# A second stacked query tile in place of a 64-row operand in the score matmuls of a banded-attention trunk

## Chip, cores and metric

The kernel runs on one core of a Trainium2 chip. The metric is device time in microseconds of one execution, taken as the median of several. Before the change it is 2212.74 us (three runs, 2210.71 to 2214.65).

## What is computed

One layer of a hybrid encoder over 2048 tokens of width 1024, in float32. Only the attention part matters here: eight heads of 64 channels, where each chunk of 64 tokens attends to itself and to the eight chunks before it.

```python
h = rms_norm(x, norm1_g); p = h @ w_in          # q, k, v, conv and pool inputs
q = rms_norm(q, q_norm_g); k = rms_norm(k, k_norm_g)
scores = einsum('bnqhd,bnkhd->bnhqk', qc, kb) * d ** -0.5
scores = where(valid, scores + bias, NEG_INF)
out = einsum('bnhqk,bnkhd->bnqhd', softmax(scores), vb)
mix = concat([out, y_conv, y_pool]);  x = x + mix @ w_out
x = x + square(relu(rms_norm(x) @ w_mlp1)) @ w_mlp2
```

The norm gains of q and k and the relative bias are scaled by 8 in the inputs, so scores are large and their products are made from split operands.

## The kernel before, in words

The tokens are handled in four blocks of 512 (`block(b, ...)`, line 332), and after them the MLP runs over everything (from line 720). A block first projects q, k and v (`project`, line 349), then runs attention, into which `weave` (line 73) mixes other matmuls: the output projection of the block before and the conv and pool projections of this block. `InOrder` (line 54) fixes the order of TensorE's instructions to the order in which they are written. The other engines' orders come from the Tile framework's scheduler, which follows priorities and its own timeline, and all DMAs on the data path are issued by SyncE (SP), in one queue.

Each float32 operand of a matmul is split into a rounded high part and the rest: hi + lo. A general product takes three matmuls (`mm3`, lines 157 to 160: hi*hi, hi*lo, lo*hi). The scores do it in two. For a head h = 2*hp + j, the keys are stacked on 128 partitions in the tile `kx`: on the head's own 64 rows the high part, on the other 64 rows the low part. `qs` stacks the queries the other way round: low part on the own rows, high part on the others. So the matmul of line 471, over 128 rows, gives q_lo*k_hi + q_hi*k_lo. Line 472 adds q_hi*k_hi with the 64 own rows of the unstacked tile `qhi` and the 64 own rows of `kx`.

`prep(hp)` (line 390) makes these tiles for a pair of heads. TensorE transposes k and q into PSUM (line 395), ScalarE writes the high part (`khi` line 399, `qhi` line 402), VectorE the low part (`klo` line 400, `qlo` line 403). Stacking is done by DMAs: the keys go to the DRAM tensor `kd` in four stores a pair (line 412) and come back as `kx` for this block and the one before (line 415); the queries go from SBUF to SBUF into `qs` in two DMAs a head (line 418). `prep` is a generator: `attention` (line 523) advances it after the first head's second, third and fourth query tile of the pair before, and `early` (line 436) makes the first pair during the v projection.

A unit of attention is one head's query tile of 128 rows, 32 units in a block. `scores` (line 460) makes the scores of up to 640 keys in PSUM: in block 0 of 128, 256, 384 or 512 keys in one bank (two matmuls), in blocks 1 to 3 always of 640 keys in two banks of 320 (four matmuls). VectorE adds the bias and takes the maximum (line 475), ScalarE the exponential (line 481). `flip` transposes the probabilities a unit later (line 492), and `values` multiplies them with v another unit later (line 507). So 3*32*4 + 32*2 = 448 score matmuls are issued, half of them by line 472.

The pool `hd` holds the tiles of the heads: `khi`, `klo` and `qlo` in one buffer each, `qhi` in two, `qs` and `kx` in two.

Of the kernel before, what the change touches and what calls it, by code (L numbers as in the profile page):

```python
# [8 lines left out]
F32 = mybir.dt.float32  # L9
F32R = mybir.dt.float32r  # L10
# [8 lines left out]
P = 128  # L19
# [7 lines left out]
TB = 512  # L27
# [16 lines left out]
ORDERED = ("PE",)  # L44
# [5 lines left out]
def follow(tc, ins, earlier):  # L50
    tc.add_manual_dep(ins, earlier, mybir.DependencyInfo(mybir.DependencyClass.NoSync, mybir.DependencyReason.DATA), reason="order")


class InOrder:
    """Instructions traced between two calls of mark() keep their order on the engines of ORDERED."""

    def __init__(self, tc):
        nc = tc.nc
# [4 lines left out]
    def mark(self):  # L63
        new = self.tc.nc.cur_bb.bb.instructions[self.seen :]
        self.seen += len(new)
        for ins in new:
            if ins.engine in self.engines:
                if ins.engine in self.last:
                    follow(self.tc, ins, self.last[ins.engine])
                self.last[ins.engine] = ins.name  # L70
# [20 lines left out]
def trunk(ctx, tc, xT, cols, cinv, w_qkv, w_cp, w_out, w1, w2, nbias, pool_w, outT):  # L91
    nc = tc.nc
    sc, ve, te, gp, sy = nc.scalar, nc.vector, nc.tensor, nc.gpsimd, nc.sync
# [12 lines left out]
    hd = high.enter_context(tc.tile_pool(name="hd", bufs=2, side="right"))  # L106

    def pd(name, tag="d"):
        if tag == "d":
            return psd.tile([P, 512], F32, tag="d", name=name)  # L110
        return psa.tile([P, 512], F32, tag=tag, bufs=3 if tag == "t" else 1, name=name)

    def pbig(name, tag):
        return psa.tile([P, 2, 512], F32, tag=tag, bufs=1, name=name)
# [17 lines left out]
    kd = dram.tile([H, P, S], F32, name="kd")  # L132
# [8 lines left out]
        return w.rearrange("p s (a b) -> p s a b", a=shape)  # L141

    class Ahead:
        """Weights of a list of loads, each brought in some places before its use."""

        def __init__(self, loads):
            self.loads, self.ready = iter(loads), []
# [23 lines left out]
        ve.tensor_tensor(out=r, in0=r, in1=t, op=ALU.mult)  # L171
        return r

# [1 line left out]
    def scratch(name):  # L175
        return scr.tile([P, 512], F32, tag="s", name=name)

# [154 lines left out]
    def block(b, prev_out):  # L332
        t0 = b * TB
# [56 lines left out]
        def prep(hp):  # L390
            nat = {}
            for nm in "kq":
                tp = pd(f"t{nm}{b}_{hp}", TK)
                for i in range(NT):
                    te.transpose(tp[:, i * P : (i + 1) * P], nrm[nm][:, i, hp * P : (hp + 1) * P], ident)
                hi = hd.tile([P, TB], F32R, tag=nm + "hi", bufs=2 if nm == "q" else 1, name=f"{nm}hi{b}_{hp}")
                lo = hd.tile([P, TB], F32R, tag=nm + "lo", bufs=1, name=f"{nm}lo{b}_{hp}")
                if nm == "k":
                    sc.copy(hi, tp)
                    ve.tensor_tensor(out=lo, in0=tp, in1=hi.bitcast(F32), op=ALU.subtract)  # L400
                else:
                    sc.activation(hi, tp, AF.Copy, scale=qgs)
                    ve.scalar_tensor_tensor(out=lo, in0=tp, scalar=qgs, in1=hi.bitcast(F32), op0=ALU.mult, op1=ALU.subtract)
                nat[nm] = (hi, lo)
                yield
            res = []
            for j in range(2):
                h = 2 * hp + j
                rows = slice(64 * j, 64 * j + 64)
                orow = slice(64 - 64 * j, 128 - 64 * j)  # L410
                for part, r in ((0, rows), (1, orow)):
                    sy.dma_start(kd[h, r, t0 : t0 + TB], nat["k"][part][rows].bitcast(F32))
                kx = hd.tile([P, 2 * TB], F32R, tag="kx", bufs=2, name=f"kx{b}_{h}")
                first = 0 if b else TB
                sy.dma_start(kx[:, first:].bitcast(F32), kd[h, :, t0 - TB + first : t0 + TB])
                qs = hd.tile([P, TB], F32R, tag="qs", bufs=2, name=f"qs{b}_{h}")
                for part, r in ((1, rows), (0, orow)):
                    sy.dma_start(qs[r].bitcast(F32), nat["q"][part][rows].bitcast(F32))
                vp = None
                if b:  # L420
                    vp = hd.tile([P, NT, 2, HD], F16, tag="vp", bufs=2, name=f"vp{b}_{h}")
                    sy.dma_start(vp.rearrange("p t s d -> p (t s d)"), vd[(b - 1) % 2, h])
                bi = hd.tile([P, 640], F32, tag="bias", bufs=2, name=f"b{b}_{h}")
                sy.dma_start(bi, bd[h])
                res.append((kx, qs, nat["q"][0][rows], rows, vp, bi))
            return res

        if b == 0:
# [7 lines left out]
        def early():  # L436
            nrm["k"] = normalize(ack, "k")
            yield
            first.extend((yield from prep(0)))
            yield  # L440
# [14 lines left out]
        sc.copy(R, rb)  # L455
        mix = po.tile([P, 2, KT, TB], F32R, tag="mix", name=f"mix{b}")

# [1 line left out]
        def scores(u, st):  # L459
            hp, j, i = u  # L460
            h = 2 * hp + j
            kx, qs, qh, rows, vp, bi = st["heads"][j]
            lo_t = max(0, 4 * b + i - 4) - (4 * b - 4)
            nk = (4 + i + 1 - lo_t) * P
            ne = 1 if nk <= 512 else 2
            hk = nk // ne
            c0 = lo_t * P
            s = pbig(f"s{b}_{h}_{i}", "s")
            for e in range(ne):
                ks = slice(c0 + e * hk, c0 + (e + 1) * hk)  # L470
                te.matmul(s[:, e, :hk], qs[:, i * P : (i + 1) * P], kx[:, ks], start=True, stop=False)  # L471
                te.matmul(s[:, e, :hk], qh[:, i * P : (i + 1) * P], kx[rows, ks], start=False, stop=True)  # L472
            sb = hd.tile([P, 640], F32, tag="sb", bufs=2, name=f"sb{b}_{h}_{i}")
            nmx = sm.tile([P, 1], F32, tag="nmx", bufs=4, name=f"nm{b}_{h}_{i}")
            ve.tensor_tensor_reduce(  # L475
                out=sb[:, :nk].rearrange("p (e k) -> p e k", e=ne),
                in0=s[:, :ne, :hk],
                in1=bi[:, 640 - nk :].rearrange("p (e k) -> p e k", e=ne),
                scale=-1.0, scalar=3.0e38, op0=ALU.add, op1=ALU.min, accum_out=nmx,
            )  # L480
            exps.append(sc.activation(sb[:, :nk], sb[:, :nk], AF.Exp, bias=nmx, scale=-1.0, accum_out=st["l"][:, i, j : j + 1]))  # L481
            return sb, lo_t, nk, vp
# [40 lines left out]
        def attention(first):  # L523
# [4 lines left out]
            for u in units + [None, None]:  # L528
                if u:
                    hp, j, i = u  # L530
                    if j == 0 and i == 0:
                        st = {"heads": ready}
                        st["l"] = sm.tile([P, NT, 2], F32, tag="l", name=f"l{b}_{hp}")
                    got = (u, st, *scores(u, st))
                else:
                    got = None
                yield 1
                if done and (u is None or (j == 1 and i == NT - 1)):
                    finish(*done)
                    done = None  # L540
                flipping = flip(*scored) if scored else None
                if flipped:
                    done = values(*flipped) or done
                flipped, scored = flipping, got
                yield 1
                if u and j == 0 and hp < H // 2 - 1:
                    if i == 1:
                        steps = prep(hp + 1)
                    if i in (1, 2):
                        next(steps)  # L550
                        yield GAP
                    elif i == 3:
                        try:
                            next(steps)
                        except StopIteration as e:
                            ready = e.value
            finish(*done)
            yield 0

# [1 line left out]
        def dense(g):  # L561
            t = pd(f"cp{b}_{g}")
            for half in range(2):
                w = weights.next()
                for kk in range(4):
                    k = half * 4 + kk
                    mm3(t, w[:, 0, kk], w[:, 1, kk], xgs[k][:, 0], xgs[k][:, 1], k == 0, k == KT - 1)
                    if kk % 2 and k < KT - 1:
                        yield
            return t  # L570
# [76 lines left out]
                mapped(j, mh)  # L647
            yield from steps

# [1 line left out]
        acc2 = po.tile([P, TB], F32, tag="acc2", name=f"acc2{b}")  # L651

        halves = [(d, half) for d in range(KT) for half in (1, 0)]
# [60 lines left out]
    for b in range(NB):  # L714
        prev_out = block(b, prev_out)
# [1 line left out]
    high.close()  # L717
    pm0 = ctx.enter_context(tc.tile_pool(name="pm0", bufs=2, space=PSUM, side="right"))

# [1 line left out]
    xp = ctx.enter_context(tc.tile_pool(name="xp", bufs=28, side="right"))  # L721
    wp = ctx.enter_context(tc.tile_pool(name="wp", bufs=WOPS, side="right"))
    rp = ctx.enter_context(tc.tile_pool(name="rp", bufs=RAWS, side="right"))
# [195 lines left out]
    for n, u in enumerate(units):  # L919
        kind, tb, c, i = u  # L920
# [84 lines left out]
```

## Time and profile before

| | |
|---|---|
| runs | 2212.74 us median, 2210.71 to 2214.65 |
| profiled execution, span from first to last instruction | 2207.5 us (the page gives no other time for it) |
| TensorE busy | 2134.6 us, 97% |
| VectorE, ScalarE, GpSimd busy | 1596.8, 1154.1, 895.8 us |
| score matmuls, line 471, busy (all forms) | 224 instructions, first at 82.9 us, last at 911.5 us |
| DMA, share of the 16 engines | 41.3% |

PE is TensorE's matmuls, PEld its weight loads (which can overlap matmuls), DVE is VectorE, ACT ScalarE, POOL GpSimd, SPq SyncE's queue. A busy time of PE adds up instructions that overlap in the pipeline, so what a matmul costs is read from the distance between the starts of neighbours, not from its own length. The four attention stretches lie at about 81 to 174, 251 to 424, 500 to 674 and 749 to 915 us.

### The profile page before, as it was taken

The numbers are of one execution on the slowest core, as the hardware profiler recorded it, in microseconds if no ns is written. First come the engines' busy times: TensorE is split into PE (matmuls) and PEld (weight loads), VectorE is DVE, ScalarE is ACT, GpSimd is POOL, SyncE is SP. The second block draws the span as 40 slices with busy tenths as digits, with TensorE's granted clock in tenths as the row PEclk, the third lists the DMA queues.
The fourth block names the chain that finished last, engine by engine and source line by source line (L and its number), as shares of the span: only waits on it lengthen the run. The fifth ranks groups of instructions, "written<-read, shape, count | busy, mean of one in ns | idle before, by whom it ended". The sixth has DMA issues, their size and how long they took to land.

```text
span 2207.5 us, 31819 instructions
## 1 busy us (share of the span) xinstructions
PE 2134.6 (97%) x11136; PEld 1266.0 (57%) x11136; DVE 1596.8 (72%) x2401; ACT 1154.1 (52%) x2163; POOL 895.8 (41%) x693
## 2 busy tenths in 40 slices
PE   8999999999999999979999979999999999999998
PEld 6777777787777777754444434444444444444443
DVE  7677556755666556797848898767877487687685
ACT  6455455635555555545646436446256464463550
POOL 4233144402211012155636556446656355363463
PEclk9999999999999999999999999999999999999999
DMA  8664665446745576352111451115521111112123
GB/s 291 184 175 144 190 218 180 145 150 201 222 145 156 168 220 182 126 196 77 55 61 58 155 189 58 58 58 203 174 76 58 59 57 61 56 52 67 58 87 114
DMA packets 156562, 285.91 MB, mean 130 GB/s; under 512 B 18545, under 2 KB 25841, under 8 KB 156401
## 3 DMA queue, kind: packets, MB, share of 16 engines
q1 hardware_dynamic: 156400, 283.88, 41.3%
q8 instruction: 87, 1.43, 0.3%
q14 instruction: 75, 0.61, 0.1%
HBM read 236.09 MB, written 39.32 MB: 125 GB/s over the span
## 4 chain that ended last, share of the span: by engine, by line
PE 65%; DVE 12%; POOL 6%; issue 6%; DMA 6%; ACT 4%; SPq 0%; POOLq 0%; DVEq 0%; ACTq 0%
PE b_d L782 18%; PE b_u L782 11%; PE a L158 4%; PE a L160 4%; PE a L159 4%; PE s L472 3%; PE cp L158 3%; PE o L158 3%; PE pt L492 2%; PE s L471 2%; PE cp L159 2%; PE cp L160 2%; DMA r_d<-w 2%; PE o L160 2%; PE o L159 2%
## 5 line engine op out<-in xcount | busy, mean ns | idle before, releaser
L782 PE MATMUL b_d<-ft_u,s_d 128*128 128x512 f16 x1152 | 264.9, 379 | 5.8 <-DVE ft_u L733 4.3
L782 PEld LDWEIGHTS <-s_u 128*128 128x128 f16 x1536 | 150.8, 98 | 202.2 <-issue 22.4
L782 PEld LDWEIGHTS <-s_d 128*128 128x128 f16 x1536 | 150.4, 98 | 191.2 <-issue 12.5
L782 PEld LDWEIGHTS <-a_d 128*128 128x128 f16 x1152 | 114.2, 99 | 158.8 <-issue 27.1
L782 PEld LDWEIGHTS <-a_u 128*128 128x128 f16 x1152 | 113.1, 98 | 146.1 <-issue 11.9
L782 PE MATMUL b_d<-fb_u,a_d 128*128 128x512 f16 x768 | 183.7, 379 | 0.5 <-DVE acc L890 0.5
L481 ACT ACTIVATE sb<-sb,nm 128x640 f32<-128x640 f32 (+4 forms) x128 | 97.6, 762 | 142.2 <-DVE nm L475 136.3
L890 DVE TENSOR_TENSOR acc<-acc,b_d 128x512 f32<-128x512 f32 x176 | 119.4, 682 | 62.5 <-PE b_d L782 62.4
L207 POOL TENSOR_TENSOR acc<-acc,sq 128x512 f32<-128x512 f32 x56 | 80.5, 1438 | 197.8 <-ACT sq L206 157.0
L158 PE MATMUL a<-wq,xg 128*128 128x512 f32 x384 | 152.4, 402 | 8.4 <-ACT wq L139 8.1
L160 PE MATMUL a<-wq,xg 128*128 128x512 f32 x384 | 154.1, 402 | 1.5 <-DVE xg L343 1.5
L159 PE MATMUL a<-wq,xg 128*128 128x512 f32 x384 | 153.4, 399 | 0.0
L475 DVE CUSTOM_DVE_ANT_0 sb<-s,b 128x640 f32<-128x640 f32 (+4 forms) x128 | 94.4, 738 | 77.2 <-PE s L472 75.2
L782 PE MATMUL b_u<-xt,s_u 128*128 128x512 f16 x576 | 132.5, 385 | 10.1 <-DVE xt L733 6.7
L494 DVE SCALAR_TENSOR_TENSOR pp<-pt,pp 128x384 f16<-128x384 f32 (+1 forms) x224 | 102.8, 485 | 49.9 <-ACT pp L493 49.5
L139 POOL CAST wc<-rwc 128x512 fp32r<-128x512 f32 x64 | 40.2, 628 | 237.7 <-PE cp L160 127.9
L284 POOL TENSOR_TENSOR pq<-pq,pq 128x512 bf16<-128x512 bf16 x32 | 38.6, 1205 | 219.4 <-ACT pq L281 219.4
L782 PE MATMUL b_u<-zt,s_u 128*128 128x512 f16 x576 | 126.9, 379 | 0.0
L754 POOL TENSOR_TENSOR s_u<-s_u,r_u 128x512 f32<-128x512 f32 x32 | 43.8, 1370 | 201.8 <-DVE s_u L736 200.4
L736 DVE SCALAR_TENSOR_TENSOR a_u<-r_u,sw,a_u 128x512 f16<-128x512 f32 x96 | 102.5, 1069 | 21.5 <-ACT a_u L735 18.8
L735 ACT ACTIVATE a_u<-r_u,sw 128x512 f16<-128x512 f32 x96 | 68.8, 719 | 93.2 <-PE b_d L782 49.5
L158 PE MATMUL o<-mix,wo 128*128 128x512 f32 x256 | 111.2, 435 | 4.0 <-DVE xo L673 4.0
(267 smaller groups left out, 5314.6 us busy)
## 6 DMA issues: line engine op xcount, KB each, us to landing
r_u<-w SPq DMA_DIRECT2D x128, 256.0 KB, 2.6
r_d<-w SPq DMA_DIRECT2D x128, 256.0 KB, 2.7
rwq<-w_qkv SPq DMA_DIRECT2D x96, 256.0 KB, 2.8
pr<-w SPq DMA_DIRECT2D x64, 256.0 KB, 3.5
rwc<-w_cp SPq DMA_DIRECT2D x64, 256.0 KB, 3.6
rwo<-w_out SPq DMA_DIRECT2D x64, 256.0 KB, 3.3
ps<-w SPq DMA_DIRECT2D x64, 256.0 KB, 3.3
kx<-kd SPq DMA_DIRECT2D x24, 512.0 KB, 5.5
```

The source lines that it names most:

```text
L158: te.matmul(out, ah, bh, start=start, stop=False)
L159: te.matmul(out, ah, bl, start=False, stop=False)
L160: te.matmul(out, al, bh, start=False, stop=stop)
L207: gp.tensor_tensor(out=acc, in0=acc, in1=q, op=ALU.add)
L472: te.matmul(s[:, e, :hk], qh[:, i * P : (i + 1) * P], kx[rows, ks], start=False, stop=True)
L475: ve.tensor_tensor_reduce(out=sb[:, :nk].rearrange("p (e k) -> p e k", e=ne), in0=s[:, :ne, :hk], in1=bi[:, 640 - nk :].rearrange("p (e k) ...
L481: exps.append(sc.activation(sb[:, :nk], sb[:, :nk], AF.Exp, bias=nmx, scale=-1.0, accum_out=st["l"][:, i, j : j + 1]))
L494: ve.scalar_tensor_tensor(out=pp[:, 1, c0:c1], in0=pt[:, :n], scalar=PSC, in1=pp[:, 0, c0:c1], op0=ALU.mult, op1=ALU.subtract)
L735: sc.activation(t[:, 0], src, AF.Copy, scale=scale)
L736: ve.scalar_tensor_tensor(out=t[:, 1], in0=src, scalar=scale, in1=t[:, 0], op0=ALU.mult, op1=ALU.subtract)
L782: te.matmul(bank, w[:, a, q * P : (q + 1) * P], xs[q][:, c], start=start and q == 0 and i == 0, stop=q == n - 1 and i == 2, skip_group_che ...
L890: ve.tensor_tensor(out=a, in0=a, in1=bk, op=ALU.add)
```

## The change

Every head gets a second stacked query tile `qx`, with the high part on its own rows and the low part on the others. The second matmul takes `qx` and all of `kx`, over 128 rows: q_hi*k_hi + q_lo*k_lo. That adds two DMAs a head (64 in the kernel) and removes the use of `qhi` and of the row slice by TensorE. The four stores of the keys are written earlier in `prep`, right after k is split. The tiles `khi`, `klo`, `qhi`, `qlo` share one tag, `nat`, with three buffers, where they had five. The diff's other lines only take out comments.

```diff
-                hi = hd.tile([P, TB], F32R, tag=nm + "hi", bufs=2 if nm == "q" else 1, name=f"{nm}hi{b}_{hp}")
-                lo = hd.tile([P, TB], F32R, tag=nm + "lo", bufs=1, name=f"{nm}lo{b}_{hp}")
+                hi = hd.tile([P, TB], F32R, tag="nat", bufs=3, name=f"{nm}hi{b}_{hp}")
+                lo = hd.tile([P, TB], F32R, tag="nat", bufs=3, name=f"{nm}lo{b}_{hp}")
...
                 nat[nm] = (hi, lo)
+                if nm == "k":
+                    for j in range(2):
+                        for part, r in ((j, slice(0, 64)), (1 - j, slice(64, 128))):
+                            sy.dma_start(kd[2 * hp + j, r, t0 : t0 + TB], (hi, lo)[part][64 * j : 64 * j + 64].bitcast(F32))
                 yield
...
-                for part, r in ((0, rows), (1, orow)):
-                    sy.dma_start(kd[h, r, t0 : t0 + TB], nat["k"][part][rows].bitcast(F32))
...
                 qs = hd.tile([P, TB], F32R, tag="qs", bufs=2, name=f"qs{b}_{h}")
-                for part, r in ((1, rows), (0, orow)):
-                    sy.dma_start(qs[r].bitcast(F32), nat["q"][part][rows].bitcast(F32))
+                qx = hd.tile([P, TB], F32R, tag="qx", bufs=2, name=f"qx{b}_{h}")
+                for t, cross in ((qs, 1), (qx, 0)):
+                    for part, r in ((cross, rows), (1 - cross, orow)):
+                        sy.dma_start(t[r].bitcast(F32), nat["q"][part][rows].bitcast(F32))
...
                 te.matmul(s[:, e, :hk], qs[:, i * P : (i + 1) * P], kx[:, ks], start=True, stop=False)
-                te.matmul(s[:, e, :hk], qh[:, i * P : (i + 1) * P], kx[rows, ks], start=False, stop=True)
+                te.matmul(s[:, e, :hk], qx[:, i * P : (i + 1) * P], kx[:, ks], start=False, stop=True)
```

With three shared buffers taken in turn, `qlo` of a pair gets the buffer of `khi` of the same pair, `khi` of the next pair that of `klo`, `klo` that of `qhi`, and `qhi` that of `qlo`.

How this moves instructions is seen on SP's queue. The first place is the start of block 1, before its attention (`rwo` are raw weights of the output projection; the last number of a name is the program's own). Before:

```order
L412 DMA kd<-khi_0_2655 64x512 x2
L412 DMA kd<-klo_0_2656 64x512 x2
L137 DMA rwo_2_1_2878<-w_out 128x512
L415 DMA kx_0_2721<-kd 128x1024
L415 DMA kx_1_2732<-kd 128x1024
L137 DMA rwo_2_0_2962<-w_out 128x512
L418 DMA qs_0_2723<-qhi_0_2698 64x512
L418 DMA qs_0_2723<-qlo_0_2699 64x512
L418 DMA qs_1_2734<-qlo_0_2699 64x512
L418 DMA qs_1_2734<-qhi_0_2698 64x512
```

The same place with the change:

```order
L408 DMA kd<-khi_0_2679 64x512 x2
L408 DMA kd<-klo_0_2680 64x512 x2
L137 DMA rwo_2_1_2908<-w_out 128x512
L417 DMA kx_0_2747<-kd 128x1024
L417 DMA kx_1_2759<-kd 128x1024
L137 DMA rwo_2_0_2996<-w_out 128x512
L422 DMA qs_0_2749<-qhi_0_2726 64x512
L422 DMA qx_0_2750<-qhi_0_2726 64x512
L422 DMA qs_0_2749<-qlo_0_2727 64x512
L422 DMA qx_0_2750<-qlo_0_2727 64x512
L422 DMA qs_1_2761<-qlo_0_2727 64x512
L422 DMA qs_1_2761<-qhi_0_2726 64x512
```

The key stores stand where they stood: the scheduler had already put them there. New are the `qx` DMAs, so that what the first head needs is complete with the fourth query DMA and no longer with the second.

The second place is VectorE at the same point of the program. Its order stays, but one instruction gains waits. Before:

```order
L400 TENSOR_TENSOR klo_0_2656<-tk_0_2650,khi_0_2655 128x512 [waits Activation_49]
L140 TENSOR_TENSOR wo_0_0_2793<-rwo_0_0_2791,wo_0_0_2793 128x512 [waits DMAHW1_49,Activation_49]
L140 TENSOR_TENSOR wo_1_1_2798<-rwo_1_1_2796,wo_1_1_2798 128x512 [waits DMAHW2_49,Activation_49]
L403 SCALAR_TENSOR_TENSOR qlo_0_2699<-tq_0_2693,qgs,qhi_0_2698 128x512 [waits Activation_49]
L140 TENSOR_TENSOR wo_1_0_2836<-rwo_1_0_2834,wo_1_0_2836 128x512 [waits DMAHW3_49,Activation_49]
```

With the change:

```order
L400 TENSOR_TENSOR klo_0_2680<-tk_0_2674,khi_0_2679 128x512 [waits Activation_49]
L140 TENSOR_TENSOR wo_0_0_2823<-rwo_0_0_2821,wo_0_0_2823 128x512 [waits DMAHW1_49,Activation_49]
L140 TENSOR_TENSOR wo_1_1_2828<-rwo_1_1_2826,wo_1_1_2828 128x512 [waits DMAHW2_49,Activation_49]
L403 SCALAR_TENSOR_TENSOR qlo_0_2727<-tq_0_2721,qgs,qhi_0_2726 128x512 [waits DMAHW4_49,DMAHW5_49,DVE_49,Activation_49]
L140 TENSOR_TENSOR wo_1_0_2866<-rwo_1_0_2864,wo_1_0_2866 128x512 [waits DMAHW3_49,Activation_49]
```

`qlo` (line 403) now waits for two DMAs, the stores of `khi`, whose buffer it takes over. TensorE's order is the same in both, with `qx` for `qhi` as the operand of the second score matmul.

## Rows read from the trace of the kernel before

**Rows 1.** The page: span, TensorE's busy time, its granted clock in 40 slices.

```profile
span 2207.5 us, 31819 instructions
...
PE 2134.6 (97%) x11136; PEld 1266.0 (57%) x11136; DVE 1596.8 (72%) x2401; ACT 1154.1 (52%) x2163; POOL 895.8 (41%) x693
...
PEclk9999999999999999999999999999999999999999
```

**Rows 2.** Windows, attention stretches: length, PE, PEld, DVE, ACT, POOL busy, PEclk, DMA.

```profile
81.00:174.00 93.00, 89.60 (x590) 67.03 (x590) 69.14 (x166) 54.89 (x135) 33.16 (x41) 0.98 0.62 180
...
251.00:424.00 173.00, 172.41 (x1212) 131.27 (x1213) 109.25 (x221) 95.65 (x208) 66.13 (x81) 1.00 0.61 190
...
500.00:674.00 174.00, 173.92 (x1197) 132.21 (x1197) 109.02 (x220) 96.62 (x234) 34.02 (x38) 0.99 0.61 186
...
749.00:915.00 166.00, 166.00 (x1147) 126.29 (x1148) 104.12 (x208) 93.83 (x232) 25.86 (x29) 1.00 0.60 179
```

**Rows 3.** Timeline of PE, one unit of block 1 after transposes: start, us, instruction.

```profile
301.34 0.39 PE L160 MATMUL o<-mix,wo 128*128 128x512 f32 x1
301.57 0.60 PE L395 MATMUL tk<-ident,nk 128*128 128x128 f32 x4
301.92 0.39 PE L471 MATMUL s<-kx,qs 128*128 128x320 f32 x1
302.25 0.41 PE L472 MATMUL s<-kx,qhi 64*128 64x320 f32 x1
...
303.27 0.50 PE L158 MATMUL o<-mix,wo 128*128 128x512 f32 x1
303.61 0.39 PE L159 MATMUL o<-mix,wo 128*128 128x512 f32 x1
303.84 0.40 PE L160 MATMUL o<-mix,wo 128*128 128x512 f32 x1
```

**Rows 4.** Timeline of PEld, the weight loads of the same unit.

```profile
302.24 0.18 PEld L472 LDWEIGHTS s<-kx,qhi 64*128 64x128 f32 x1 [0.16 <-issue]
...
303.38 0.19 PEld L159 LDWEIGHTS o<-mix,wo 128*128 128x128 f32 x1
```

**Rows 5.** Timeline of PE, a unit of block 1 after a projection matmul.

```profile
323.01 0.39 PE L160 MATMUL o<-mix,wo 128*128 128x512 f32 x1
323.24 0.30 PE L471 MATMUL s<-kx,qs 128*128 128x320 f32 x1
...
324.50 0.50 PE L158 MATMUL o<-mix,wo 128*128 128x512 f32 x1
```

**Rows 6.** Timeline of PE, units of block 0 with 512 keys and with 128.

```profile
102.51 0.39 PE L471 MATMUL s<-kx,qs 128*128 128x512 f32 x1
...
103.25 0.44 PE L492 MATMUL pt<-ident,sb 128*128 128x128 f32 x2
...
105.30 0.22 PE L471 MATMUL s<-kx,qs 128*128 128x128 f32 x1
...
105.70 0.44 PE L492 MATMUL pt<-ident,sb 128*128 128x128 f32 x2
```

**Rows 7.** Waits of PE, whole kernel: us in total, times, longest.

```profile
PE s L471 <- DMA qs<-qlo: 3.4, 3, 1.3
```

**Rows 8.** SP's timeline at the start of block 1, and line 418 in that window.

```profile
245.38 1.12 SPq L418 DMA_DIRECT2D qs<-qlo  x2
...
DMA to landing us min/median/max: 5.4/5.8/5.9
```

**Rows 9.** DMA issues of the whole kernel: count, size, median us to landing.

```profile
qs<-qhi SPq DMA_DIRECT2D x32, 128.0 KB, 5.2
```

**Rows 10.** SP and DVE, one preparation in block 1; landing of its stores.

```profile
302.90 1.11 SPq L412 DMA_DIRECT2D kd<-khi  x2
...
310.37 0.75 DVE L403 SCALAR_TENSOR_TENSOR qlo<-tq,qgs,qhi 128x512 fp32r<-128x512 f32 x1
...
DMA to landing us min/median/max: 3.7/3.8/3.9
```

More of the change, by code (lines that the diff above doesn't have):

```diff
@@ L424, in prep @@
                 sy.dma_start(bi, bd[h])
-                res.append((kx, qs, nat["q"][0][rows], rows, vp, bi))
+                res.append((kx, qs, qx, vp, bi))
             return res
@@ L461, in scores @@
             h = 2 * hp + j
-            kx, qs, qh, rows, vp, bi = st["heads"][j]
+            kx, qs, qx, vp, bi = st["heads"][j]
             lo_t = max(0, 4 * b + i - 4) - (4 * b - 4)
```

## Prediction

> **What bounds the kernel now.** I read the page first. PE is busy for 2134.6 of 2207.5 us, at the higher of its two clock levels (2.4 GHz) nearly throughout [rows 1]. An average over stages with different limits says little, so the second view is the table of windows over the four attention stretches, the only places where score matmuls run [rows 2]. In blocks 1 to 3 PE is busy for 172.41 of 173, 173.92 of 174 and 166.00 of 166 us, while DVE, the next engine, has 109.25 of 173 us (63%), ACT 55% and DMA 0.61. There a microsecond taken off PE should be a microsecond off the end. In block 0 PE has 89.60 of 93 us and DVE 69.14, so the cover is thinner. The waits say the same: the one wait before a score matmul that a DMA ends costs 3.4 us in three pieces in the whole kernel [rows 7].
>
> Busy does not mean at its peak, so the third view is the timeline of single matmuls, by the distance of their starts. Projection matmuls of 512 columns follow each other at 303.61 and 303.84, so 0.23 us apiece [rows 3]. The score matmuls have only 320 columns, yet L471 starts at 301.92 and L472 at 302.25: 0.33 us for fewer columns. The four and the step to the next L158 at 303.27 take 1.35 us [rows 3]. The loads tell why. The load of L472, marked 64*128, begins only at 302.24, after an idle 0.16 us that waits for nothing the profile shows, together with the start of its matmul. The load of L159 begins at 303.38, inside L158, which runs from 303.27 to 303.77 [rows 3, 4]. So a load is hidden where both neighbours use 128 rows, and exposed where 64 and 128 rows meet. That happens on entering every L472 and on leaving it, twice for each. The step from L160 into L471, 128 rows both, shows no such gap: 323.01 to 323.24, the usual 0.23 [rows 5]. It is the switch that costs, not the score matmul as such.
>
> **The change, part by part.** *Matmuls.* Their number, columns and order stay; L472 becomes a 128-row matmul, so no switch is left. What a 320-column matmul between equals costs is not in the trace, and I bound it. Below: four transposes of 128 columns take 0.35 us (301.57 to 301.92), 0.09 each. Above: 0.23 for 512 columns [rows 3]. By columns, 0.23*320/512 is 0.144; on the line between the two rows it is 0.16. I take 0.15. One rule is weighed here. The Trainium skill, TensorE: Matmul & The Clock Gate, section Back-to-back issue gap, gives columns/2.4 ns plus 2.5 ns at full clock, which is an estimate of 0.136 us for 320 columns and would make the saving below 5 us larger. By the same formula 512 columns take 0.216 us, and the trace shows 0.23 [rows 3], so I stay with the rows.
>
> Blocks 1 to 3 have 96 units. A unit that follows L160 takes 1.26 us from its first start to the next L158 (323.24 to 324.50) [rows 5]; one that follows transposes takes 1.35 [rows 3]. New: 4*0.15 = 0.60. I take the smaller saving, 0.66, for all: 96*0.66 = 63.4 us. Block 0 has 32 units of two matmuls. With 512 keys a unit takes 102.51 to 103.25, 0.74 us, and would take 2*0.23 = 0.46; with 128 keys 0.40 becomes about 2*0.09 = 0.18 [rows 3, 6]. The savings are 0.28 and 0.22, 0.25 in the mean: 8.0 us. Together 71.4 us of PE time.
>
> *The added DMAs.* 64 DMAs of 128 KB, as the `qs` DMAs are [rows 9]. SP spends 1.12 us on two [rows 8], so 0.56*16 = 9 us a block, spread over a stretch of 150 us. Within attention a pair's tiles are loaded a whole pair ahead, so they are hidden; the cover is some four units of 4.6 us, and if it went, each of the 32 heads would show its landing. At the start of a block it is short. The first scores of block 1 already wait for `qs`, and they will now wait for the fourth query DMA instead of the second. That is two issues later, 1.1 us, less what the landings overlap; they take 5.4 to 5.9 us behind the big `kx` loads [rows 8]. Between 0 and 1.2 us each, I take 0.7: three blocks show this wait [rows 7], so 2.1 us.
>
> *The shared buffers.* `qlo` now waits on DVE until the stores of `khi` have landed. Queued behind it are DVE's low halves of weights and the bias step L475, for which ACT and then PE wait. In block 1 the stores are issued from 302.90 on, the second by about 303.4, and land up to 3.9 us later, at 307.3; `qlo` starts at 310.37 [rows 10]. That leaves 3 us, of which a faster PE takes less than one. The other three takeovers reach back by a pair, over 10 us. Cost nothing here; without this slack it would be a rival below. The key stores, written earlier in the code, stand at the same place of SP's queue: nothing.
>
> *Cover.* PE shrinks by 21 us in each of blocks 1 to 3. DVE's 109.25 us then lie in about 152, 72%; DMA goes from 0.61 to about 0.72. What is late next is DVE, but it is still far off. In block 0, 69.14 us lie in 85, 81%, and units there are half as long, so I count 2 of the 8 us as lost in waits on DVE (between none and all 8).
>
> *Sum.* 71.4 - 2.1 - 2.0 = 67.3 us. The profiled execution's span goes from 2207.5 to 2140.2. The median of the runs stands 5.2 us above that span (2212.74), and the same 5.2 on top gives 2145.4: **2145 us**.
>
> **The rivals.** *The load stays too long for its cover.* The load of L472 is recorded at 0.18 us and those of its 128-row neighbours at 0.19 [rows 4], and 320 columns take 0.15. If the loads can't overlap one another, the pace is 0.19, a unit 0.76: 96*0.50 = 48, and about 5 in block 0, less 4: 2164 us. Against it: transposes with a load each run at 0.09 [rows 3].
>
> *The cover goes.* If each of the 128 units then waits 0.2 us more for DVE or a DMA, 26 us come back: 2171 us. For it: queues run in order, and everything moves closer. Against it: DVE at 72%.
>
> *No load can be hidden between equals.* The Trainium skill, TensorE: Matmul & The Clock Gate, section The mechanism, says that a weight load overlaps running matmuls only when their row groups differ. As a mechanism of this kernel: two neighbours that use the same 128 rows would always show the load, the change would turn the switches into such pairs, a unit would stay at 1.26 us, and the added DMAs would be all that is left, 2 to 4 us: 2216 us, no change. Against it: the load of L159 runs inside L158 on the same 128 rows [rows 4]. By that rule the trace disagrees.
>
> *Slower: `qlo` blocks DVE.* If the stores of `khi`, queued among more DMAs, land late, DVE stands at `qlo` in each of 16 preparations, and L475 with it. It decides from 71.4/16 = 4.5 us a preparation on; at 6 us it is 96 - 67 = 29 us above now: 2242 us. For it: landings of up to 5.9 us at a block's start [rows 8]. Against it: it would need them some 7 us later than now, with 3 us of slack first [rows 10].
>
> **How the numbers follow.** The forecast has 0.84, the pace of 0.19 has 0.05, the lost cover 0.06, the rule of equal rows 0.02, the blocked DVE 0.03. The forecast's own bounds: at 0.144 a matmul, the 18 units that follow `prep`'s transposes (two for each pair that a block prepares within attention) at their full 0.75, and no give-back, 75 us, 2137; at 0.17 and all of block 0 lost, 63.4 - 7.7 - 2.1 = 54 us, 2159. Some 3 us of scatter of the median come on top below, and the first rival is taken in above: **2134 to 2165 us**. A measurement of this kernel can tell about 0.2%, 4.4 us, from no change. Faster: 0.84 + 0.05 + 0.06 = 0.95. The same: 0.02. Slower: 0.03.
>
> **What would show it.** Right: the second score matmul is marked 128*128, its load starts before the matmul ahead ends, the idle 0.16 before it is gone, and score matmuls of 320 columns start 0.14 to 0.17 us apart; the attention stretches of blocks 1 to 3 shrink by about 21 us each, that of block 0 by 6, and nothing else changes length. The first score matmuls of blocks 1 to 3 wait for `qx`, 0.5 to 1.2 us longer. Wrong: starts 0.19 or 0.34 apart; new PE waits on L475, L494 or weights within attention of over 10 us in total; DVE idle before `qlo` that a DMA of `khi` ends; or a stage outside attention that grows by what attention lost.

## The result, and the profile after

The change takes 2160.39 us (median of four runs, 2159.07 to 2171.22) against 2211.72 us for the kernel before beside it: a ratio of 0.977, 95% interval 0.9749 to 0.979. That is 51 us saved where 67 were forecast. The profiled execution took 2161.39 us, and its span of 2159.6 us lies 47.9 under that of [rows 1]. So 19 us of the sum are missing by the spans (16 by the medians: this time 1.8 us lie around the span, where 5.2 were assumed; in the later runs of the kernel before it is 1.8 as well), and the runs below look for them.

The page of the changed kernel, in the lines of [rows 1]:

```profile
span 2159.6 us, 31956 instructions
...
PE 2063.0 (96%) x11136; PEld 1266.4 (59%) x11136; DVE 1604.8 (74%) x2401; ACT 1154.1 (53%) x2163; POOL 902.0 (42%) x693
...
PEclk9999999999999999989999999999999999999999
```

PE's busy time fell by 2134.6 - 2063.0 = 71.6 us. What PE is not busy is span less busy time: 72.9 us before, 96.6 now, 23.7 more. The two make the 47.9. The saving is all there, and a third of it came back as idle time of PE.

The windows over the four attention stretches, with the columns of [rows 2]:

```profile
81.00:171.50 90.50, 82.01 (x592) 68.48 (x591) 69.67 (x166) 55.63 (x136) 33.66 (x41) 0.94 0.71 210
248.00:409.00 161.00, 152.87 (x1212) 132.02 (x1213) 110.29 (x223) 96.61 (x208) 67.95 (x81) 0.96 0.75 220
484.00:644.00 160.00, 151.70 (x1198) 131.22 (x1199) 108.69 (x222) 98.45 (x235) 34.88 (x38) 0.97 0.73 216
717.00:876.00 159.00, 150.13 (x1188) 129.83 (x1188) 105.07 (x217) 97.77 (x240) 26.94 (x29) 0.98 0.69 205
```

PE was busy for practically all of blocks 1 to 3; now 8 to 9 us of each are not. The granted clock, 0.99 to 1.00 there before, is 0.96 to 0.98. From the start of a block's first score matmul to the end of its last, worked out from the traces, the four blocks took 87.8, 164.6, 165.5 and 163.7 us, and take 85.1, 150.5, 151.0 and 148.7.

The pace is as forecast. PE's timeline of one unit of block 1, and PEld's (as [rows 3, 4]):

```profile
299.96 0.39 PE L475 MATMUL s<-kx,qs 128*128 128x320 f32 x1
300.19 0.31 PE L476 MATMUL s<-kx,qx 128*128 128x320 f32 x1
300.34 0.31 PE L475 MATMUL s<-kx,qs 128*128 128x320 f32 x1
300.49 0.31 PE L476 MATMUL s<-kx,qx 128*128 128x320 f32 x1
300.64 0.39 PE L158 MATMUL o<-mix,wo 128*128 128x512 f32 x1
...
300.05 0.19 PEld L476 LDWEIGHTS s<-kx,qx 128*128 128x128 f32 x1
300.20 0.19 PEld L475 LDWEIGHTS s<-kx,qs 128*128 128x128 f32 x1
```

Between the later ones of these starts lie 0.15 us, and the load of L476 at 300.05 runs inside the matmul that began at 299.96. The unit takes 0.68 us, 1.35 before [rows 3].

The idle time shows in the view of groups by line, PE, 81 to 912 us (busy, mean ns of one, then idle before and what ended it):

```profile
L496 PE MATMUL pt<-ident,sb 128*128 128x128 f32 x560 | 84.6, 277 | 9.5 <-DVE pp L498 9.3
L475 PE MATMUL s<-kx,qs 128*128 128x320 f32 (+1 forms) x224 | 73.6, 335 | 9.7 <-DMA qs<-qhi 5.8 <-DVE nm L479 2.8 <-DMA qs<-qlo 1.1
...
L511 PE MATMUL y<-v,pp 128*128 128x64 f16 x960 | 50.7, 194 | 5.6 <-DVE pp L498 5.1 <-ACT pp L497 0.5
L395 PE MATMUL tq<-ident,nq 128*128 128x128 f32 x60 | 10.2, 296 | 9.2 <-DVE r1t L170 6.1 <-DVE klo L400 3.1
```

In the same view of the kernel before, these four groups had 0.5, 4.1, 2.2 and 0.2 us of idle time, 7 in all; now they have 34. Two of them, before:

```profile
L492 PE MATMUL pt<-ident,sb 128*128 128x128 f32 x550 | 81.3, 274 | 0.5 <-ACT sb L481 0.5
...
L395 PE MATMUL tq<-ident,nq 128*128 128x128 f32 x60 | 9.2, 275 | 0.2 <-DVE klo L400 0.2
```

Three places make up most of the 34.

**Block starts** (7.1 us for query DMAs, 3.4 before [rows 7]) and **the first preparation in block 0**. From the timelines of PE and DVE:

```profile
250.49 0.38 PE L475 MATMUL s<-kx,qs 128*128 128x320 f32 x1 [2.70 <-DMA qs<-qhi]
...
720.23 0.61 PE L475 MATMUL s<-kx,qs 128*128 128x320 f32 x1 [3.06 <-DMA qs<-qhi]
...
92.77 0.75 DVE L403 SCALAR_TENSOR_TENSOR qlo<-tq,qgs,qhi 128x512 fp32r<-128x512 f32 x1 [2.10 <-DMA kd<-khi]
...
96.45 0.55 PE L511 MATMUL y<-v,pp 128*128 128x64 f16 x7 [3.17 <-DVE pp L498]
```

**The preparation in the third pair of heads of blocks 1 to 3** is the largest: six waits of 16.4 us together, nearly all that L496 and L395 show. Beside attention ScalarE measures the MLP's weights (`survey`, lines 265 to 301): 128 loads of 256 KB, `pr` and `ps`, go through three buffers, and each is squared in ACT's order between two exponentials. In block 1 the timelines of ACT, DVE and PE read:

```profile
336.09 0.63 ACT L281 ACTIVATE pq<-pr 128x512 bf16<-128x512 f32 x1 [5.62 <-DMA pr<-w]
336.62 0.74 ACT L497 ACTIVATE pp<-pt 128x384 f16<-128x384 f32 x2
...
337.12 0.89 DVE L498 SCALAR_TENSOR_TENSOR pp<-pt,pp 128x384 f16<-128x384 f32 x2 [5.67 <-ACT pp L497]
...
342.12 0.68 DVE L400 TENSOR_TENSOR klo<-tk,khi 128x512 fp32r<-128x512 f32 x1
...
337.74 1.33 PE L496 MATMUL pt<-ident,sb 128*128 128x128 f32 x5 [2.53 <-DVE pp L498]
...
342.94 1.09 PE L395 MATMUL tq<-ident,nq 128*128 128x128 f32 x4 [3.07 <-DVE klo L400]
```

Read it from the top: ACT stands 5.62 us before a square whose load has not landed. Behind the square in ACT's order is the eviction L497. DVE's L498 waits for that, PE's transposes wait for DVE, and 5 us later PE waits again, for `klo`, which ACT's `khi` and DVE's preparation delayed in their turn. ACT's groups for the squares show the source:

```profile
L298 ACT ACTIVATE pt<-ps 128x512 bf16<-128x512 f32 x64 | 39.5, 618 | 15.6 <-DMA ps<-w 15.6
...
L281 ACT ACTIVATE pq<-pr 128x512 bf16<-128x512 f32 x64 | 37.3, 618 | 9.2 <-DMA pr<-w 9.2
```

That is 24.8 us of ACT's time, against 3.6 (2.2 and 1.4) in this view of the kernel before:

```profile
L298 ACT ACTIVATE pt<-ps 128x512 bf16<-128x512 f32 x64 | 39.4, 617 | 2.2 <-DMA ps<-w 2.2
...
L281 ACT ACTIVATE pq<-pr 128x512 bf16<-128x512 f32 x64 | 36.8, 617 | 1.5 <-DMA pr<-w 1.4
```

Three waits, one in the third pair of each of blocks 1 to 3, make up 14.2 of the 24.8: 5.62, 5.41 and 3.18 us.

### The profile page after: what moved, and what is told of

It is laid out like the page before. It is cut to its first block, busy times and chain, and to the rows that moved or that the text cites. A ratio compares the mean times of both kernels' runs of the same rounds, so it can differ in the third digit from the quotient of the medians.

```text
span 2159.6 us, 31956 instructions
## 1 busy us (share of the span) xinstructions
PE 2063.0 (96%) x11136; PEld 1266.4 (59%) x11136; DVE 1604.8 (74%) x2401; ACT 1154.1 (53%) x2163; POOL 902.0 (42%) x693
## 4 chain that ended last, share of the span: by engine, by line
PE 58%; DVE 13%; DMA 9%; issue 7%; POOL 7%; ACT 4%; SPq 1%; POOLq 0%; DVEq 0%; ACTq 0%
PE b_d L786 19%; PE b_u L786 8%; PE a L160 4%; PE a L158 4%; PE a L159 4%; PE cp L158 2%; PE pt L496 2%; DMA r_d<-w 2%; PE cp L159 2%; PE cp L160 2%; POOL t1u L770 2%; PE o L158 2%; DVE ft_u L737 2%; PE o L160 2%; PE y L511 2%
## 5 line engine op out<-in xcount | busy, mean ns | idle before, releaser
L498 DVE SCALAR_TENSOR_TENSOR pp<-pt,pp 128x384 f16<-128x384 f32 (+1 forms) x224 | 102.5, 483 | 67.1 <-ACT pp L497 66.3
L139 POOL CAST wc<-rwc 128x512 fp32r<-128x512 f32 x64 | 40.5, 633 | 204.5 <-PE cp L160 94.7
L140 DVE TENSOR_TENSOR wq<-rwq,wq 128x512 fp32r<-128x512 f32 x96 | 74.7, 788 | 51.1 <-ACT wq L139 50.9
```

Source lines behind the costliest of these rows:

```text
L140: (lo or ve).tensor_tensor(out=w[:, 1], in0=raw, in1=w[:, 0].bitcast(F32), op=ALU.subtract)
L498: ve.scalar_tensor_tensor(out=pp[:, 1, c0:c1], in0=pt[:, :n], scalar=PSC, in1=pp[:, 0, c0:c1], op0=ALU.mult, op1=ALU.subtract)
```

## The experiments

All were timed in five rounds beside the kernel before. Theory A: the 64 added DMAs cost what is missing. B: the faster PE by itself outruns DVE, ACT and the loads. C: the shared buffers do. D: the survey's loads come too late for a faster PE. E: ACT's two table loads in a preparation (1.28 us each) do. F, G and H stand in the expectations that use them.

**The pace without the added DMAs.** The kernel before, with line 472 reading `qs` again; it leaves out q_hi*k_hi.

```diff
-te.matmul(s[:, e, :hk], qh[:, i * P : (i + 1) * P], kx[rows, ks], start=False, stop=True)
+te.matmul(s[:, e, :hk], qs[:, i * P : (i + 1) * P], kx[:, ks], start=False, stop=True)
```

> The kernel before, with one line changed: the second score matmul reads qs and kx over all 128 rows, as the first does (so the product of the two high parts is left out and the cross products are added twice). No DMA, no tile and no buffer is changed. Theory A, the added DMAs take back what is missing: the whole PE saving of about 71 us shows, 2141 us (2136 to 2148), and PE waits less than 10 us in the four attention stretches. Theory B, the faster PE by itself outruns DVE, ACT and the loads: about 2160 us as in the change, with some 30 us of PE waits there.

Measured: 2157.04 us, ratio 0.9743 [0.9729, 0.9758]. Without one added DMA, and with the old buffers, it is almost as slow as the change, so A falls as the main cause, and the time is near the 2160 of B. The third pair stalls as well. Block 3, the timelines of ACT and SP:

```profile
793.62 0.63 ACT L298 ACTIVATE pt<-ps 128x512 bf16<-128x512 f32 x1 [7.51 <-DMA ps<-w]
...
782.85 0.42 SPq L674 DMA_DIRECT2D x2d<-xo  x1
789.64 0.33 SPq L672 DMA_DIRECT2D xo<-xT  x1
790.07 0.38 SPq L296 DMA_DIRECT2D ps<-w  x1
```

SP's waits, 775 to 790 us (in total, times, longest):

```profile
SPq L672 <- DMA x2d<-xo: 10.3, 2, 6.3
```

SP issues a store of the residual tile `xo` at 782.85 and then nothing for 6.4 us: the next `xo` load needs the store's buffer and waits for its landing, and the survey's load stands behind it in the queue.

**The same, with 64 dead DMAs to DRAM added** (128 KB each, from the halves of q; it leaves out q_hi*k_hi too).

```diff
+                for part, r in ((0, rows), (1, orow)):
+                    sy.dma_start(qd[h, r], nat["q"][part][rows].bitcast(F32))
```

> The kernel of e1_same_rows with 64 DMAs more, two a head, of 64 rows by 512 values each from the high and the low part of q into a DRAM tensor that nothing reads (the product of the two high parts is left out as in e1_same_rows). Theory A: most of what is missing comes back, 2153 to 2163 us, with ACT standing for a survey load in the third pair of blocks 1 to 3. Theory B: within 3 us of e1_same_rows.

Measured: 2161.12 us, 0.9765 [0.9747, 0.9782]. The point estimate for the DMAs is 4 us; the intervals overlap, so it is not told apart from nothing.

**The change with four shared buffers** (`nat` with `bufs=4`; the accumulator `vacc` shares the tag `acc` to make room).

> The change, with four buffers instead of three under the tag nat, so that khi, klo, qhi and qlo each have their own (the room comes from vacc, which takes the buffer of acc). Theory C, the shared buffers are part of the loss: DVE no longer stands 2.1 us at qlo in block 0, PE's 3.2 us behind it and the half clock of 6.8 us go, 5 to 8 us faster than the change, 2152 to 2156 us. Theories A and B: that wait goes too, but the total stays within 3 us of the change, 2157 to 2163.

Measured: 2162.38 us, 0.9758 [0.9742, 0.9774]. DVE's idle time before `qlo` in block 0 is gone, and PE's wait behind it falls from 3.17 to 1.26 us, but the time does not fall. C is seen in the trace and not in the result.

**128 rows without a second stacked tile**: the high part of q in zero-padded tiles, one for each head, written by ACT straight into place.

```diff
+                    for j in range(2):
+                        r = slice(64 * j, 64 * j + 64)
+                        sc.activation(hi[j][r], tp[r], AF.Copy, scale=qgs[r])
+                        ve.scalar_tensor_tensor(out=lo[r], in0=tp[r], scalar=qgs[r], in1=hi[j][r].bitcast(F32), op0=ALU.mult, op1=ALU.subtract)
```

> The kernel before, where ScalarE writes the high part of q for each head into a tile of 128 rows of its own whose other 64 rows are zero for good; the second score matmul reads that tile and all of kx. No DMA is added, ACT and DVE get 16 instructions more each (about 11 us), klo keeps its buffer, khi and qlo share one. Theory A: 2141 to 2150 us, below the change. Theory B: about 2160 us. If a 128-row load were dear whatever stands in the rows, the pace of score matmuls would not be 0.15 us.

Measured: 2168.23 us, 0.9794 [0.9775, 0.9812]. The 64 DMAs are saved, 16 instructions each are added on ACT and DVE in the preparations where PE waits for these engines, and the stalls stay (L501 and L402, which answer to L496 and L395, have 10.1 and 9.7 us of idle time). No gain.

**The survey without its loads**, in the change and in the kernel before; the squares read a constant, so the weights' norms are left out.

```diff
-                raw = scr.tile([P, 512], F32, tag="x", bufs=3, name=f"pr{ft}_{half}")
-                sy.dma_start(raw, w1[ft, half])
+                raw = ones.broadcast_to([P, 512])
```

> The change, with the survey of w1 and w2 squaring a constant row instead of loaded weights: its 128 loads of 256 KB are left out, ScalarE's squares stay (so the MLP's scales are not those of the weights). Theory D, PE stands in the third pair of blocks 1 to 3 because ScalarE, in its order, waits for a survey load that stands behind another DMA on SP: that standing goes, PE's waits there fall from 5 to 7 us a block to 0 to 4, the half clock after them goes, 2136 to 2150 us. Theory E, the square root's table loads and the chain on DVE behind them are the cause: ScalarE's wait goes but PE's does not, 2155 to 2162 us.

> The kernel before with the same survey without loads (the scales are not those of the weights). Theories D and E: PE is not held by these loads before, so 2206 to 2214 us; if it falls as far as e5_after_still does against the change, the loads cost the same in both and don't explain the missing part.

Measured: the change falls to 2134.73 us, 0.9661 [0.9645, 0.9677]; the kernel before stays at 2210.96 us, 0.9999 [0.9988, 1.001]. The change without the loads, its page:

```profile
PE 2054.7 (96%) x11136; PEld 1260.1 (59%) x11136; DVE 1601.6 (75%) x2401; ACT 1153.5 (54%) x2163; POOL 904.0 (42%) x693
```

Its groups by line, PE, 81 to 912 us:

```profile
L494 PE MATMUL pt<-ident,sb 128*128 128x128 f32 x560 | 82.6, 273 | 0.2 <-ACT sb L483 0.2
...
L393 PE MATMUL tq<-ident,nq 128*128 128x128 f32 x60 | 9.2, 275 | 2.1 <-DVE r1t L170 1.1 <-DVE klo L398 1.0
```

The two groups of the third pair lose 9.3 + 7.1 = 16.4 us of idle time, and PE's busy time falls by another 8.3: the stretches at half clock that lay at the three stalls (the one in block 1 is shown in the last section) are gone. Together that is 24.7, and the span fell by 24.1. Blocks 1 to 3 now take 143.3, 140.1 and 141.8 us, 21 to 25 under the kernel before, where 21 were forecast. This much of D is shown: the same loads cost the old kernel nothing and the new one some 25 us. That they do it by coming late, and not by the traffic that goes with them, is read from the chain above (the idle time that went is that of the two groups behind ACT's wait) and not from this pair of runs.

**No root in the residual's norm** (a copy instead, so that its table is not loaded; the output differs).

> The change, with a copy in place of the square root in the second norm's statistics of blocks 0 to 2 (the root is left out, so the scale of the MLP's input differs): two table loads of 1.28 us on ScalarE fall away in the third pair of blocks 1 to 3, the rest of the chain stays. Theory E: PE's waits there fall by 4 us or more a block, 2145 to 2152 us. Theory D: ScalarE stands for the load as before and only the wait of the transposes of q gets shorter, by 1 to 3 us a block, 2152 to 2159 us.

Measured: 2162.43 us, 0.9786 [0.977, 0.9801], with eight table loads in the blocks instead of 14. E falls; the 2152 to 2159 that theory D gave for this kernel was missed as well.

**Which wait makes the loads late?** Five kernels, on the change (`follow` places an instruction behind another in the order; parts of the edits are left out); all_three is xo_kx_late with survey_on_pool:

```diff
# xo_on_pool: the residual's loads on GpSimd's queue
-                    sy.dma_start(xr, xT[d * P : (d + 1) * P, t0 : t0 + TB])
+                    gp.dma_start(xr, xT[d * P : (d + 1) * P, t0 : t0 + TB])
# xo_late: on SP, but behind the query DMAs of the own block's first pair
+                    follow(tc, sy.dma_start(xr, xT[d * P : (d + 1) * P, t0 : t0 + TB]).ins, pairs[-1].ins.name)
# xo_kx_late: xo_late, four buffers, and the second head's kx behind the first head's queries
+                if j:
+                    follow(tc, load.ins, last_q.ins.name)
# survey_on_pool: the survey's loads on GpSimd's queue
-                sy.dma_start(raw, w1[ft, half])
+                gp.dma_start(raw, w1[ft, half])
```

> The change, with the loads of xo (the residual rows of the output projection, 256 KB each) issued by GpSimd instead of SP; everything is computed. Theory D, the survey load is late because on SP it stands behind such a load, which waits for a store to land: ScalarE's wait in the third pair shrinks from 5 us or more to under 2, 2145 to 2155 us. If the survey load is late for another reason (SP's eight outstanding DMAs, slow landings): within 3 us of the change.

> The change, with each load of the residual tiles xo placed in SP's queue behind the last query DMA of its own block's first pair, so that the first xo loads of the next block no longer stand ahead of the survey's loads pr and ps; nothing else is changed. Theory D (the missing time is the third pair of each block, where PE waits behind DVE behind ACT for a survey load that SP issues late, because an xo load ahead of it in SP's queue waits for a store to land): ACT's gaps before L281 and L282 near 336, 571 and 805 us fall from 3.2 to 5.6 us to under 2 us, the half-clock stretches of 10.2 us there shrink to 3.4 or go, and the time is 2143 to 2153 us, 7 to 17 us under the change. Rival F (the loads themselves are slow because so many DMAs are under way, and whichever stands first in the queue makes no difference): the gaps stay above 3 us and the time is within 3 us of the change's 2160.

> The kernel of e12_xo_late with two more edits: the key load kx of the second head of a pair is placed behind the query DMAs of the first head, and the low and high halves of queries and keys share four buffers instead of three (the accumulator vacc gives its space). Theory G (the block starts and the wait for qlo in block 0 are the rest of the missing time): PE's waits at the three block starts, 2.7, 1.3 and 3.1 us in the change, fall to under 1.5 us each, the 3.2 us in block 0 fall to about 1, and the time is 3 to 8 us under that of e12_xo_late. Rival H (these waits are absorbed later, or the landing of the last query DMA does not depend on the big load ahead of it): within 2 us of e12_xo_late.

> The change, with the survey's loads pr and ps issued by GpSimd instead of SP; nothing else is changed. Theory D, put more narrowly (not the residual tiles alone: whatever stands ahead of a survey load in SP's queue and waits for a landing makes the load late): the loads leave SP's queue, ACT's gaps of 3.2 to 5.6 us before L281 and L298 in the third pair of blocks 1 to 3 fall under 1.5 us each, the half-clock stretches of 10.2 us there go, and the time is 2138 to 2150 us, under the 2152 of the kernel that moves only the xo loads and near the 2135 of the kernel without survey loads. Rival F (the landings are slow whoever issues them, for the traffic): the gaps stay over 2.5 us and the time is over 2152. Against both, GpSimd's own queue could hold a load up behind a cast of weights; then the gaps would be ended by DMA pr or ps but the issue would stand late on GpSimd.

> The kernel of e13_xo_kx_late (late xo loads, late second kx load, four shared buffers) with the survey's loads issued by GpSimd as well: an attempt at a version that beats both kernels. If the survey loads are the larger part of what was missing and the block starts the smaller one, 2134 to 2146 us; if the block starts are worth nothing, as e13 against e12 made it look, within 2 us of e14_survey_on_pool.

| kernel | us | ratio, interval |
|---|---|---|
| e9_xo_on_pool | 2152.11 | 0.9738 [0.9723, 0.9754] |
| e12_xo_late | 2155.33 | 0.975 [0.973, 0.977] |
| e13_xo_kx_late | 2154.81 | 0.975 [0.9728, 0.9772] |
| e14_survey_on_pool | 2156.18 | 0.9757 [0.9741, 0.9774] |
| e15_all_three | 2160.43 | 0.9766 [0.9747, 0.9786] |

With the `xo` loads on GpSimd, ACT waits for survey loads 8.4 us, not 24.8:

```profile
L298 ACT ACTIVATE pt<-ps 128x512 bf16<-128x512 f32 x64 | 39.4, 617 | 7.1 <-DMA ps<-w 7.0
...
L281 ACT ACTIVATE pq<-pr 128x512 bf16<-128x512 f32 x64 | 37.0, 617 | 5.8 <-POOL pq L284 4.4 <-DMA pr<-w 1.4
```

This is the fastest kernel that still computes everything, though its interval touches that of the change. The stall has in part moved and not gone. GpSimd now stands in front of its own `xo` load until a store has landed; DVE waits 4.71 us for a cast of weights (L139) that stands behind that load, and PE waits for DVE at a new place of the third pair, 4.41 us in block 1 and 7.3 us in blocks 1 to 3 together. The timelines of GpSimd and PE:

```profile
330.85 0.56 POOL L676 DMA_DIRECT2D xo<-xT  x1 [6.91 <-DMA x2d<-xo]
...
335.54 0.80 PE L158 MATMUL cp<-xg,wc 128*128 128x512 f32 x1 [4.41 <-DVE ms_0c L214]
```

Moving `xo` back on SP took ACT's long wait out of block 1 and left the others. ACT's timeline of e12_xo_late:

```profile
561.29 0.63 ACT L299 ACTIVATE pt<-ps 128x512 bf16<-128x512 f32 x1 [3.94 <-DMA ps<-w]
...
795.03 0.63 ACT L299 ACTIVATE pt<-ps 128x512 bf16<-128x512 f32 x1 [3.79 <-DMA ps<-w]
```

So an `xo` load is not all that holds SP up. In the change itself, the loads whose landing ended ACT's waits of 5.62, 5.41 and 3.18 us were issued at 331.30, 566.10 and 800.59 us, each within 0.1 us of the landing of a head's key load `kx`. SP had issued that key load eight DMAs earlier, and two of the seven between are the new ones into `qx`. SP's waits, 325 to 336, 556 to 567 and 790 to 801 us:

```profile
SPq L279 <- DMA kx<-kd: 1.1, 1, 1.1
...
SPq L296 <- DMA kx<-kd: 2.2, 1, 2.2
...
SPq L296 <- DMA kx<-kd: 1.9, 1, 1.9
```

These key loads took 7.0 to 7.8 us to land, and the survey's loads behind them 4.4 to 4.7. In blocks 2 and 3 of e12_xo_late it is the same: `kx` landed at 556.56 and 790.40, and the loads that ACT then waited for were issued at 556.62 and 790.46. Why SP waits for that landing, and what it costs, no run here shows.

In e13_xo_kx_late the first scores of blocks 1 to 3 wait 1.8 us in all (longest 0.6), not 7, and yet its time is that of e12_xo_late: rival H, as far as intervals of 4 us can tell. PE's wait in block 0, which theory G put at about 1 us there, stays at 3.17, although DVE no longer stands in front of `qlo`.

e14_survey_on_pool takes the loads out of SP's queue altogether, and they still land late. The timelines of GpSimd (a pair of loads) and ACT:

```profile
793.05 1.09 POOL L296 DMA_DIRECT2D ps<-w  x2 [3.15 <-issue]
...
799.41 0.63 ACT L298 ACTIVATE pt<-ps 128x512 bf16<-128x512 f32 x1 [4.97 <-DMA ps<-w]
```

Its DMA issues, 246 to 912 us (count, size, median us to landing):

```profile
ps<-w POOLq DMA_DIRECT2D x64, 256.0 KB, 4.1
```

The load that ACT waits for there was issued at 793.05 and landed at 799.33: 6.3 us, among the key and query loads of a head. GpSimd had stood 3.15 us before it issued the pair, for nothing that the profile shows, so a part of the lateness may lie there. Both conditions of rival F came true, gaps of over 2.5 us and a time over 2152, and the missed expectation of e15_all_three says that the cures do not add up. So the queue's order is one part of the lateness (e9, block 1 of e12, the `kx` waits above) and the landing time behind a burst of loads another; their shares stay open. An earlier issue, from a fourth survey buffer, was not tried.

## Why the prediction was right in sign and range, and 15 us too low

- **Pace: right.** Mostly 0.144 to 0.149 us between starts where 0.15 was taken. The sum over all runs of score matmuls, from the first start to the start of the next instruction, went from 144.6 to 73.7 us: 70.9, forecast 71.4. By the Trainium skill, TensorE: Matmul & The Clock Gate, section Back-to-back issue gap, an estimate was 0.136, with a formula that the page gives for a single matmul by itself. The trace lies nearer the 0.144 of the scaled row. By the Trainium skill, the same page, section The mechanism, a weight load overlaps running matmuls only when their row groups differ, and there would have been no gain. The trace disagrees: the load at 300.05 is hidden.
- **Added DMAs: the size.** 2.1 us were put on block starts, 0 to 1.2 each. The waits for query DMAs grew by 7.1 - 3.4 = 3.7 us, one of them to 3.06; without the added DMAs, in e1_same_rows, they are 3.2. Nearly all of it is spent on `qs`, and not on `qx` as was said (0.2 us). No head later in a block shows a landing, as said. e3_more_dmas puts all DMAs at some 4 us, uncertain.
- **Shared buffers: a wrong reading.** The slack of 3 us was read from one preparation in block 1 [rows 10] and taken for all. In block 0, where a preparation has less time, DVE stood 2.10 us before `qlo` and PE 3.17 behind it, and in the first preparations within blocks 1 and 2 DVE stood 0.4 and 1.2 us there for a store of the keys. "Nothing" was false of the trace, though e2_four_buffers found no time in it. Block 0 shrank by 2.7 us where 6 were counted; with the old buffers it shrank by 5.5 and 6.0 (82.3 us in e1_same_rows, 81.8 in e3_more_dmas), but with four buffers by 4.1 and 2.7 (83.7 in e2, 85.1 in e13), so the buffers' part is likely and not shown.
- **Cover: the step that failed.** "What is late next is DVE, but it is still far off" judged the cover by busy shares. What was late next was a load: the survey's, in front of ACT's evictions. The step gave back 2 us; measured, the survey costs some 25. Neither the queue of SP in a whole pair nor what stands in ACT's order had been read. Without those loads the change lands at 2134.73, 10 us under the forecast, so nothing else is needed for the 15 that are missing.
- **The rivals.** "The cover goes" came nearest in kind. Its 26 us are near the 25 of the survey's loads, but its time of 2171 us is 11 above the measured one, and its shape was wrong: not 0.2 us in each of 128 units, but 0.6 to 4.1 us at two places in each of blocks 1 to 3. The warning sign named for it, PE waits of over 10 us within attention, came true. Loads of 0.19 did not set the pace, and `qlo` held DVE up three times, for 3.7 us in all, and not in each of 16 preparations.
- **The range: luck in part.** The forecast's own upper bound was 2159 us. The measured 2160.39 lies in the stated range because that was widened to 2165 for loads of 0.19, which did not come; the loss that did come was not in it.

## What to carry to other kernels

Here neighbouring matmuls with the same rows hide one another's weight loads, and a 64-row operand between them did not; look for operands of half the rows between full ones, and pad or restack them. Before counting a faster bottleneck in full, go through the in-order queues of the engines beside it, not their busy shares: find each instruction that waits for a load just in time, above all background work put in front of the main path, and see how much earlier it would be wanted. A load that is moved to another engine's queue takes its own wait along, so look at what stands behind it there.

## What was not expected of the hardware

A stop of PE costs more than its length. Windows of the change around two stops (PE busy first, the granted clock third from the end):

```profile
93.10:95.10 2.00, 0.18 (x2) 0.06 (x2) 2.00 (x3) 0.38 (x1) 1.84 (x3) 0.99 0.68 187
95.10:101.90 6.80, 5.45 (x31) 4.62 (x32) 4.81 (x16) 1.97 (x6) 1.33 (x2) 0.50 0.88 283
...
252.10:255.50 3.40, 3.40 (x9) 2.65 (x8) 1.06 (x3) 1.54 (x3) 0.00 (x0) 0.50 1.04 357
337.40:347.60 10.20, 6.79 (x35) 5.91 (x36) 8.69 (x20) 6.41 (x11) 4.27 (x6) 0.50 0.63 183
```

During or just after the stops that end at 96.45, 250.49 and 337.74 us the granted clock falls to 0.50, the lower level of 1.2 GHz, for 3.4 to 10.2 us. The matmuls of 512 columns then start 0.43 us apart, not 0.23: eight of them after 252.1 lose 1.6 us on top of the 2.70 of the stop. The prediction had no term for this. And the survey's loads, unchanged in number and size, took a median of 3.9 to 4.0 us to land in blocks 1 to 3 where they had taken 3.1 to 3.3: the same traffic and 48 DMAs more, in less time.
